# A decoder layer whose recurrent outputs go to two halves of the partitions, with GpSimd's tile arithmetic on VectorE and another meter for side work

## The chip, the core and the metric

One core of a Trainium2 chip runs the whole kernel. The metric is the device time of one execution in microseconds (us). A kernel is timed several times and the median is given; beside it stands one execution taken by the hardware profiler, from which all rows of the profile come.

## The reference

One decoder layer in float32 on 256 tokens of width 2048. A residual stream `x` passes three branches, each with a norm before and after:

```python
h = rms_norm(x, mix_pre_norm)
proj = h @ w_in                                  # 2048 x 10536
# mLSTM, 4 heads, from q, k, v, o and two gates  -> ha
# RWKV-7, 16 heads of 64: per token
#   S = S diag(w) - (S kk) (kk a)^T + v k^T ;  y = S r
# group norm of y, bonus, output gate            -> hb
merged = sigmoid(g_a) * (ha @ w_branch_a) + sigmoid(g_b) * (hb @ w_branch_b)
x = x + rms_norm(merged @ w_out, mix_post_norm)
x = x + rms_norm(cross_attention(rms_norm(x), rms_norm(mem)), xattn_post_norm)
u = rms_norm(x, ffn_pre_norm) @ w_up             # 2048 x 16384
uc = conv_b + causal_conv3(u)
x = x + rms_norm((gelu(uc_gate) * uc_up) @ w_down, ffn_post_norm)
```

## The kernel before

**The big products.** All weights are streamed from HBM in tiles of 128 x 1024 numbers (512 KB; 128 x 768 in the first block `sm`). To keep float32 precision, each number is split into a high part (ScalarE's cast to fp32r, tile `wh`, line 348) and a low part (VectorE's subtraction, tile `wl`, line 357); the activations are split likewise (`hh`/`hl`, `qh`/`ql`, `fh`/`fl`, `as`). Three TensorE products (high x high, high x low, low x high) add up in one PSUM bank. `raw`, the tile as loaded, has three buffers, `wh` and `wl` four each. TensorE's products, the side ones too, are all issued by the helper `mm` at line 181. In `fm` blocks a product has 256 columns (outputs by feature), in `tm` blocks 512 (by token).

**The order of the work.** `blocks` lists the big products: `sm` (small columns of `w_in`), `r`, `k`, `v` (two blocks each), `q` (two), `vm` and `o` (two each, `tm`), then the gates and branch products in turn, `w_mo`, the cross-attention products, 32 blocks `w_fu` and two `w_fd`. `run()` walks through them. For each weight tile it issues the split of the tile three ahead and the load of the tile six ahead, then TensorE's products of this one. A weight tile of an `fm` block is two half steps of 12 products each.

**Side work.** Everything else (scaling a block's result, gates, norms, the RWKV recurrence, softmax, residuals) is written as generators, and `yield` ends a piece. `Spread.half()` is called at every half step and decides which pieces are issued there. There are three lists: `bulk` (what follows a block, in order), `back` (long preparations: `sm_rest`, four `k_group`, `bonus`, `inverses`, `hb_split`) and `chains` (one piece each `chain` half steps: `gates`, `rwkv`, the squares of a residual). `Meter` books a price for each VectorE and ScalarE instruction (VectorE 70 + 1.04 ns an element, ScalarE 200 + 0.83). `half()` adds `RATE_D` and `RATE_A` to the two credits up to `CAP`; one piece of `bulk` or `back` is issued if both credits are above zero; a piece that books nothing passes on to the next in line. Chains run while both credits are above -700. GpSimd's work isn't booked. `side.need` and `side.until` issue a task's pieces at once where a block needs the result. Engines run their instructions in the order of issue, so a side product on TensorE that waits for VectorE holds the big products behind it.

**The places that the change touches.**

- `x_piece` (line 459) splits two rows of `x` and lets GpSimd square them and add them up (lines 464 to 468) for the first norm, whose row of rstd comes in `sm_evac` by `st0.finish`.
- `sm_rest` makes the low-rank decay and gate products (`zwa`) of RWKV; `gates` the mLSTM gates and the tile `pw`.
- `k_group` (lines 740 to 752) makes for two feature tiles the scaled vectors of the recurrence: `KR` and `BK`, in part on GpSimd. `head_sums` makes sums over a head by a TensorE product of a split tile (side products `ssk`, `bon`).
- `inverses` inverts the 32 x 32 triangular blocks, 31 steps of two VectorE instructions, two steps a piece.
- `rwkv(hf)` runs for each half of the heads over four chunks of 64 tokens, a step each three half steps: transposes (`bkt`) and `gram`, then `lv`, `X`, `U`, and last `Tn` (the next state) and `Y` (the output). `aux` is the pool of four side PSUM buffers. Of the two heads `e` of a pair, Tn goes to partitions `E2[e]` (0 to 63 or 64 to 127); Y goes for both heads to the partitions of the chunk, `cr = E2[c % 2]`, in two buffers `qy[e]`.
- `Residual` adds a branch to `x`, in eight parts: scale `z`, add to `xr` (GpSimd for parts 2 to 7), split into the next block's input. In the first residual (`early`, for the cross-attention) each part's square is added by GpSimd at once; in the second (for `w_fu`) the squares follow as a chain.
- `fd_evac` writes the result; one of eight pieces goes over ScalarE and GpSimd.

Of the kernel before, what the change touches and what calls it, by code (L numbers as in the profile page):

```python
# [15 lines left out]
P = 128  # L16
# [54 lines left out]
class Spread:  # L71


    RATE_D, RATE_A, CAP = 600.0, 820.0, 1200.0
# [28 lines left out]
    def half(self):  # L103
        self.tick += 1
        self.cd = min(self.cd + self.RATE_D, self.CAP)
        self.ca = min(self.ca + self.RATE_A, self.CAP)
# [39 lines left out]
def _layer(ctx, tc, nc, d, dbg):  # L146
# [95 lines left out]
    class Stat:  # L242
# [14 lines left out]
        def add(self, src, eng=None):  # L257
            if self.n == 0:
                self.start()
                act.activation(self.acc, src, AF.Square)  # L260
            else:
                q = self.square()
                act.activation(q, src, AF.Square)
                (eng or dve).tensor_add(self.acc, self.acc, q)  # L264
            self.n += 1
# [193 lines left out]
    def x_piece(c):  # L459
        for j in range(2):  # L460
            split_gain(hh[:, c * 2 + j], hl[:, c * 2 + j], xq[c][:, j], pcol("mixg", c * 2 + j))
        if c == 0:
            st0.start()
            pool.tensor_mul(st0.acc, xq[c], xq[c])
        else:
            q = st0.square()
            pool.tensor_mul(q, xq[c], xq[c])
            pool.tensor_add(st0.acc, st0.acc, q)
        st0.n += 1
# [4 lines left out]
    def pre_sm(ci, feed):  # L474
# [8 lines left out]
        if ci + 3 < 8:  # L483
            x_piece(ci + 3)
        if ci == 4:
            sp.dma_start(con, d["con"])
# [21 lines left out]
    def sm_evac(ps):  # L508
        dve.tensor_scalar(om, pcol("mu", 0, 27), -1.0, 1.0, op0=ALU.mult, op1=ALU.add)
        dve.tensor_scalar(oka, pcol("ka", 0, 8), -1.0, 1.0, op0=ALU.mult, op1=ALU.add)  # L510
        yield from st0.finish(3)
# [19 lines left out]
    def sm_rest(wa, gl0, gl1):  # L531
# [3 lines left out]
        for i, h in enumerate(hid):  # L535
# [5 lines left out]
            dve.tensor_sub(ul[E2[i]], up[E2[i]], uh[E2[i], i])  # L541
            yield
# [28 lines left out]
    def gates():  # L571
# [92 lines left out]
        for o in (0, 256):  # L664
            for e in range(2):
                v = pw[E2[e], :, o + e * 64:o + e * 64 + 64]
                pool.tensor_mul(v, v, bc(ccol("im", 64)[E2[e]], 4))
# [40 lines left out]
    def k_group(p0):  # L708
# [31 lines left out]
        pool.tensor_mul(KR8[:, :, 1], f8(rr[:, ss]), f8(ep))  # L740
# [4 lines left out]
        pool.tensor_mul(k2, kr, k2)  # L745
# [4 lines left out]
        for e in range(2):  # L750
            dve.tensor_mul(BK8[E2[e], :, e], f8(kk)[E2[e]], f8(nr)[E2[e]])
            pool.tensor_mul(BK8[E2[e], :, 1 - e], f8(k2)[E2[e]], f8(nr)[E2[e]])
# [5 lines left out]
    def head_sums(name, v):  # L758
# [4 lines left out]
        for _ in range(3):  # L763
# [7 lines left out]
    def inverses():  # L771
# [38 lines left out]
        act.copy(Lt, L.rearrange("p c i -> p i c"))  # L810
        yield
# [47 lines left out]
    def rwkv(hf):  # L859
# [12 lines left out]
        for c in range(4):  # L872
# [5 lines left out]
            if c < 3:  # L878
# [3 lines left out]
                act.copy(bkt, q)  # L882
            au = C("au", f"au{hf}", [P, 2, 2, 4, 64])
# [55 lines left out]
            qy = [aux("Y", [P, 4, 64]) for _ in range(2)]  # L939
            for j, e in heads():  # L940
                mm(qy[e][cr, j], gr[:, e, j], uv[:, e, j], start=(j == 0), stop=(c == 0))
            if c:
                for j, e in heads():
                    mm(qy[e][cr, j], KR[E2[e], p0 + j, c, 1], T[hf][E2[e], j], start=False)
            for e in range(2):
                act.copy(ye[cr, e], qy[e][cr])
# [92 lines left out]
    def mlstm():  # L1039
        pw, vm, so = M["pw"], M["vm"], M["so"]  # L1040
        M["pws"] = T2("pws")
        pool.tensor_add(M["pws"].rearrange("p a b -> p (a b)").rearrange("p (h q) -> p h q", h=4),
                        pw[:, :, 128:256], pw[:, :, 256:384])
# [143 lines left out]
    class Residual:  # L1187
# [8 lines left out]
        def run(self):  # L1196
# [27 lines left out]
            def add(i, eng):  # L1224
                eng.tensor_add(part(xr, i), part(xr, i), part(z, i))  # L1225
# [11 lines left out]
            for i in range(1, 8):  # L1237
                if i == 1:
                    add(1, dve)
                if i < 7:  # L1240
                    scale(i + 1)
                    add(i + 1, pool)
# [3 lines left out]
                if self.early:  # L1246
                    self.st2.add(part(xr, i - 1), pool)
                elif i == 6:
                    self.stats = side.add(self.squares(0), chain=1)
                yield  # L1250
            if self.early:
                self.stats = side.add(self.squares(7), chain=1)
                yield

        def squares(self, i0):
            for i in range(i0, 8):
                self.st2.add(part(M["xr"], i), pool)
# [312 lines left out]
    def fd_evac(n):  # L1570

        def gen(ps):
# [19 lines left out]
            def result(t, c):  # L1592
                f = slice(c % 2 * 512, c % 2 * 512 + 512)
                x, z_ = M["xt"][c // 2][:, t, f], M["z3", c // 2][:, t, f]
                if t and c == 1:
                    act.activation(z_, z_, AF.Copy, scale=rco[:, t:t + 1])
                    pool.tensor_add(x, x, z_)
                else:
                    dve.scalar_tensor_tensor(x, z_, rco[:, t:t + 1], x, op0=ALU.mult, op1=ALU.add)
# [124 lines left out]
```

## Time and profile before

| what | value |
|---|---|
| median of 3 runs | 1940.54 us (1940.47 to 1940.81) |
| profiled execution, its time | 1939.58 us |
| its span, first to last instruction | 1937.6 us |
| TensorE (PE) busy | 1900.6 us, 98% |
| VectorE (DVE) busy | 1326.1 us, 68% |
| ScalarE (ACT) busy | 1001.6 us, 52% |
| GpSimd (POOL) busy | 137.1 us, 7% |
| read from HBM | 347.73 MB, 181 GB/s over the span |
| mean granted TensorE clock | 0.995 |

A row of a group reads: line, engine, operation, out<-in, shapes, xcount, then busy us and mean ns of one, then the engine's idle time just ahead of it and who ended it. A row of a timeline begins with its start and its duration; merged rows carry a count. Overlapping instructions are merged, so a row's duration is up to the last one's end. A row of stretches reads `A:B length, busy time of each engine (xinstructions)`, then the granted TensorE clock, the share of the DMA engines and GB/s; narrowed to one engine it has that engine's time alone. A row of the chain of waits has start, duration and what it was.

### The profile page before, as it was taken

The numbers are of one execution on the slowest core, as the hardware profiler recorded it, in microseconds if no ns is written. First come the engines' busy times: TensorE is split into PE (matmuls) and PEld (weight loads), VectorE is DVE, ScalarE is ACT, GpSimd is POOL, SyncE is SP. The second block draws the span as 40 slices with busy tenths as digits, with TensorE's granted clock in tenths as the row PEclk, the third lists the DMA queues.
The fourth block names the chain that finished last, engine by engine and source line by source line (L and its number), as shares of the span: only waits on it lengthen the run. The fifth ranks groups of instructions, "written<-read, shape, count | busy, mean of one in ns | idle before, by whom it ended". The sixth has DMA issues, their size and how long they took to land.

```text
span 1937.6 us, 36532 instructions
## 1 busy us (share of the span) xinstructions
PE 1900.6 (98%) x15084; PEld 1798.7 (93%) x15084; DVE 1326.1 (68%) x1789; ACT 1001.6 (52%) x1434; POOL 137.1 (7%) x127
## 2 busy tenths in 40 slices
PE   7999999999999999899999999999999999999998
PEld 7999987999999999789999999999999998888886
DVE  7879886566566665867767666776667675556555
ACT  4776535544454565555555445544455454455553
POOL 4213100010100000304000000000000000000000
PEclk9999999999999999999999999999999999999999
DMA  6555555344465675435555555556555555655554
GB/s 200 177 163 165 185 164 162 110 142 142 157 183 185 209 261 185 157 133 171 182 186 191 195 196 192 191 190 200 191 194 189 195 195 195 215 192 192 194 195 152
DMA packets 97606, 352.20 MB, mean 182 GB/s; under 512 B 10880, under 2 KB 11136, under 8 KB 97056
## 3 DMA queue, kind: packets, MB, share of 16 engines
q1 hardware_dynamic: 96496, 348.07, 55.0%
q8 instruction: 118, 1.93, 0.4%
q10 hardware_dynamic: 720, 1.15, 0.2%
q0 software_dynamic: 224, 0.66, 0.1%
q14 instruction: 48, 0.39, 0.1%
HBM read 347.73 MB, written 2.10 MB: 181 GB/s over the span
## 4 chain that ended last, share of the span: by engine, by line
PE 87%; DVE 5%; ACT 2%; issue 2%; DMA 2%; POOL 1%; DVEq 0%; SPq 0%; ACTq 0%; POOLq 0%
PE fm L181 59%; PE tm L181 23%; DVE wl L357 2%; ACT wh L348 1%; DMA raw<-in_w_in_dram 1%; DVE fl L66 1%; PE Y L181 1%; DMA raw<-in_w_fu_dram 0%; PE gram L181 0%; PE lv L181 0%; DVE z L66 0%; POOL xr L1225 0%; POOL stx L264 0%; DMA x<-in_x_dram 0%; DVE BK L66 0%
## 5 line engine op out<-in xcount | busy, mean ns | idle before, releaser
L357 DVE TENSOR_TENSOR wl<-raw,wh 128x1024 fp32r<-128x1024 f32 (+1 forms) x648 | 809.6, 1251 | 448.5 <-ACT wh L348 445.4
L348 ACT CAST wh<-raw 128x1024 fp32r<-128x1024 f32 (+1 forms) x648 | 675.7, 1046 | 562.1 <-PE fm L181 373.2
L181 PE MATMUL fm<-fl,wh 128*128 128x256 f32 x2048 | 568.3, 278 | 1.0 <-DVE fl L66 1.0
L181 PE MATMUL fm<-fh,wh 128*128 128x256 f32 x2048 | 568.7, 278 | 0.2 <-ACT fh L66 0.2
L181 PE MATMUL fm<-fh,wl 128*128 128x256 f32 x2048 | 567.7, 277 | 0.0
L181 PEld LDWEIGHTS fm<-fl,wh 128*128 128x128 f32 x2048 | 386.0, 188 | 1.8 <-DVE fl L66 1.7
L181 PEld LDWEIGHTS fm<-fh,wh 128*128 128x128 f32 x2048 | 386.0, 188 | 0.5 <-ACT fh L66 0.5
L181 PEld LDWEIGHTS fm<-fh,wl 128*128 128x128 f32 x2048 | 386.0, 188 | 0.0
L181 PE MATMUL tm<-wh,as 128*128 128x512 f32 x1024 | 315.5, 389 | 0.0
L181 PE MATMUL fm<-hh,wl 128*128 128x256 f32 x1072 | 301.7, 281 | 11.9 <-DVE wl L357 11.9
L181 PE MATMUL fm<-hh,wh 128*128 128x256 f32 x1072 | 305.5, 285 | 1.1 <-ACT wh L348 1.1
L181 PE MATMUL fm<-hl,wh 128*128 128x256 f32 x1072 | 300.7, 280 | 0.0
L181 PEld LDWEIGHTS tm<-wh,as 128*128 128x128 f32 x1024 | 192.1, 188 | 39.8
L181 PEld LDWEIGHTS fm<-hh,wl 128*128 128x128 f32 x1072 | 203.8, 190 | 13.8 <-DVE wl L357 13.8
L181 PEld LDWEIGHTS fm<-hh,wh 128*128 128x128 f32 x1072 | 204.0, 190 | 4.1 <-ACT wh L348 1.5
L181 PEld LDWEIGHTS fm<-hl,wh 128*128 128x128 f32 x1072 | 204.2, 190 | 0.1
L181 PE MATMUL tm<-wl,as 128*128 128x512 f32 x512 | 199.3, 389 | 0.0
L181 PEld LDWEIGHTS tm<-wl,as 128*128 128x128 f32 x512 | 96.1, 188 | 20.0
L66 ACT CAST as<-ac 128x256 fp32r<-128x256 f32 x128 | 45.6, 404 | 112.9 <-PE tm L181 112.9
L66 DVE TENSOR_TENSOR as<-ac,as 128x256 fp32r<-128x256 f32 x128 | 48.6, 422 | 61.7 <-ACT as L66 61.6
L225 POOL TENSOR_TENSOR rco<-var,mhalf 128x1 f32<-128x1 f32 x2 | 1.1, 551 | 1011.6 <-DVE var L66 1011.6
L181 PE MATMUL fm<-mgh,wh 128*128 128x256 f32 x256 | 71.4, 279 | 0.0
(363 smaller groups left out, 2323.6 us busy)
## 6 DMA issues: line engine op xcount, KB each, us to landing
raw<-in_w_fu_dram SPq DMA_DIRECT2D x256, 512.0 KB, 4.2
raw<-in_w_in_dram SPq DMA_DIRECT2D x160, 512.0 KB, 3.7
raw<-in_w_fd_dram SPq DMA_DIRECT2D x128, 512.0 KB, 4.2
raw<-in_w_br_dram SPq DMA_DIRECT2D x32, 512.0 KB, 3.8
raw<-in_w_mo_dram SPq DMA_DIRECT2D x32, 512.0 KB, 4.3
raw<-in_w_xk_dram SPq DMA_DIRECT2D x8, 512.0 KB, 4.5
raw<-in_w_xq_dram SPq DMA_DIRECT2D x8, 512.0 KB, 3.6
raw<-in_w_xv_dram SPq DMA_DIRECT2D x8, 512.0 KB, 4.1
```

The costliest lines, as they stand in the source:

```text
L66: return f(out, *a, **k)
L181: pe.matmul(out, lhsT, rhs, start=start, stop=stop, skip_group_check=True)
L225: pool.tensor_tensor(out, v, mhalf[:, 0:out.shape[1]], op=ALU.pow)
L348: nc.scalar.copy(wh, r)
L357: nc.vector.tensor_sub(wl, r, self.st[self.nl][0])
```

## The change

It does seven things: (1) Y of both heads goes to one PSUM buffer, each head to its own half of the partitions, and ScalarE's copies bring both to the chunk's rows; (2) the tile arithmetic of GpSimd (squares and sums of squares, residual adds, parts of `k_group`, masks of `pw`, `pws`, one result) goes to VectorE, its squares to ScalarE, and is booked there; the small powers for rstd, copies and fills stay on GpSimd; (3) squares of the first norm come later, those of the first residual as a chain after part 6; (4) `RATE_D` rises from 600 to 740, and a credit below -700 is lifted to -700 ahead of each half step's addition; (5) more empty pieces stand ahead of side products: six for three in `head_sums`, five ahead of `zwa`; (6) a piece ends between `bkt` and `gram`; (7) the copy `Lt` is cut in two pieces.

```diff
@@ class Spread @@
-    RATE_D, RATE_A, CAP = 600.0, 820.0, 1200.0
+    RATE_D, RATE_A, CAP, DEBT = 740.0, 820.0, 1200.0, -700.0
@@ Spread.half @@
         self.tick += 1
-        self.cd = min(self.cd + self.RATE_D, self.CAP)
-        self.ca = min(self.ca + self.RATE_A, self.CAP)
+        self.cd = min(max(self.cd, self.DEBT) + self.RATE_D, self.CAP)
+        self.ca = min(max(self.ca, self.DEBT) + self.RATE_A, self.CAP)
@@ Stat.add @@
-        def add(self, src, eng=None):
+        def add(self, src):
...
                 act.activation(q, src, AF.Square)
-                (eng or dve).tensor_add(self.acc, self.acc, q)
+                dve.tensor_add(self.acc, self.acc, q)
@@ x_piece @@
             split_gain(hh[:, c * 2 + j], hl[:, c * 2 + j], xq[c][:, j], pcol("mixg", c * 2 + j))
-        if c == 0:
-            st0.start()
-            pool.tensor_mul(st0.acc, xq[c], xq[c])
-        else:
-            q = st0.square()
-            pool.tensor_mul(q, xq[c], xq[c])
-            pool.tensor_add(st0.acc, st0.acc, q)
-        st0.n += 1
@@ pre_sm @@
             x_piece(ci + 3)
+        else:
+            for c in range((ci - 5) * 2, (ci - 5) * 2 + 2):
+                st0.add(xq[c])
@@ sm_evac @@
         dve.tensor_scalar(oka, pcol("ka", 0, 8), -1.0, 1.0, op0=ALU.mult, op1=ALU.add)
+        for c in (6, 7):
+            st0.add(xq[c])
+            yield
@@ sm_rest @@
             dve.tensor_sub(ul[E2[i]], up[E2[i]], uh[E2[i], i])
             yield
+        for _ in range(5):
+            yield
@@ gates @@
                 v = pw[E2[e], :, o + e * 64:o + e * 64 + 64]
-                pool.tensor_mul(v, v, bc(ccol("im", 64)[E2[e]], 4))
+                dve.tensor_mul(v, v, bc(ccol("im", 64)[E2[e]], 4))
@@ k_group @@
         dve.tensor_mul(kk, kk, nr)
-        pool.tensor_mul(KR8[:, :, 1], f8(rr[:, ss]), f8(ep))
+        dve.tensor_mul(KR8[:, :, 1], f8(rr[:, ss]), f8(ep))
...
         pool.tensor_copy(pce[:, ss], ep.rearrange("p a (c t) -> p a c t", c=4)[:, :, :, 63])
-        pool.tensor_mul(k2, kr, k2)
+        dve.tensor_mul(k2, kr, k2)
...
             dve.tensor_mul(BK8[E2[e], :, e], f8(kk)[E2[e]], f8(nr)[E2[e]])
-            pool.tensor_mul(BK8[E2[e], :, 1 - e], f8(k2)[E2[e]], f8(nr)[E2[e]])
+            dve.tensor_mul(BK8[E2[e], :, 1 - e], f8(k2)[E2[e]], f8(nr)[E2[e]])
@@ head_sums @@
         split(h, l, v)
-        for _ in range(3):
+        for _ in range(6):
@@ inverses @@
         Lt = C("Lt", "au1", [P, 32, 32])
-        act.copy(Lt, L.rearrange("p c i -> p i c"))
-        yield
+        for i in (slice(0, 16), slice(16, 32)):
+            act.copy(Lt[:, i], L.rearrange("p c i -> p i c")[:, i])
+            yield
@@ rwkv: bkt and gram @@
                 act.copy(bkt, q)
+                yield
@@ rwkv: Y @@
             ye = ysb.rearrange("p (a b) v -> p b a v", b=2)
-            qy = [aux("Y", [P, 4, 64]) for _ in range(2)]
+            qy = aux("Y", [P, 4, 64])
             for j, e in heads():
-                mm(qy[e][cr, j], gr[:, e, j], uv[:, e, j], start=(j == 0), stop=(c == 0))
+                mm(qy[E2[e], j], gr[:, e, j], uv[:, e, j], start=(j == 0), stop=(c == 0))
...
                 for j, e in heads():
-                    mm(qy[e][cr, j], KR[E2[e], p0 + j, c, 1], T[hf][E2[e], j], start=False)
+                    mm(qy[E2[e], j], KR[E2[e], p0 + j, c, 1], T[hf][E2[e], j], start=False)
             for e in range(2):
-                act.copy(ye[cr, e], qy[e][cr])
+                act.copy(ye[cr, e], qy[E2[e]])
@@ mlstm @@
         M["pws"] = T2("pws")
-        pool.tensor_add(M["pws"].rearrange("p a b -> p (a b)").rearrange("p (h q) -> p h q", h=4),
-                        pw[:, :, 128:256], pw[:, :, 256:384])
+        dve.tensor_add(M["pws"].rearrange("p a b -> p (a b)").rearrange("p (h q) -> p h q", h=4),
+                       pw[:, :, 128:256], pw[:, :, 256:384])
@@ Residual.run: add @@
-            def add(i, eng):
-                eng.tensor_add(part(xr, i), part(xr, i), part(z, i))
+            def add(i):
+                dve.tensor_add(part(xr, i), part(xr, i), part(z, i))
@@ Residual.run, squares @@
                 if i == 1:
-                    add(1, dve)
+                    add(1)
...
                     scale(i + 1)
-                    add(i + 1, pool)
+                    add(i + 1)
...
                     side.more()
-                if self.early:
-                    self.st2.add(part(xr, i - 1), pool)
-                elif i == 6:
-                    self.stats = side.add(self.squares(0), chain=1)
-                yield
-            if self.early:
-                self.stats = side.add(self.squares(7), chain=1)
-                yield
-        def squares(self, i0):
-            for i in range(i0, 8):
-                self.st2.add(part(M["xr"], i), pool)
+                if i == 6:
+                    self.stats = side.add(self.squares(), chain=1)
+                yield
+        def squares(self):
+            for i in range(8):
+                self.st2.add(part(M["xr"], i))
@@ fd_evac: result @@
                 x, z_ = M["xt"][c // 2][:, t, f], M["z3", c // 2][:, t, f]
-                if t and c == 1:
-                    act.activation(z_, z_, AF.Copy, scale=rco[:, t:t + 1])
-                    pool.tensor_add(x, x, z_)
-                else:
-                    dve.scalar_tensor_tensor(x, z_, rco[:, t:t + 1], x, op0=ALU.mult, op1=ALU.add)
+                dve.scalar_tensor_tensor(x, z_, rco[:, t:t + 1], x, op0=ALU.mult, op1=ALU.add)
```

## Prediction

> **What bounds the kernel now.** I read the page's first part, then busy time by stretches of 20 us or a stage, then each engine's timeline in the stretches where TensorE loses time.
>
> ```profile
> PE 1900.6 (98%) x15084; PEld 1798.7 (93%) x15084; DVE 1326.1 (68%) x1789; ACT 1001.6 (52%) x1434; POOL 137.1 (7%) x127
> 1040.00:1240.00 200.00, 200.00 (x1761) 200.00 (x1760) 138.32 (x186) 100.39 (x129) 0.00 (x0) 1.00 0.58 192
> 6.70:66.00 59.30, 48.24 (x370) 45.94 (x370) 44.40 (x50) 30.46 (x46) 21.37 (x16) 0.94 0.62 186
> 100.00:300.00 200.00, 196.99 (x1527) 184.76 (x1527) 168.26 (x246) 110.62 (x149) 38.10 (x33) 1.00 0.54 168
> ```
>
> TensorE bounds it. From 1040 us on it takes a 256-column product every 200/1761 = 0.1136 us without a break, and nothing that the change does to the other engines can show there. Time can come from two things only: fewer or quicker TensorE instructions, and the stretches where TensorE starves. The worst of those is the head: 370 products in 59.3 us are worth 42 us, so 17 are lost. Others, shown below, lie around 425, 790-810 and 865-920 us. Except at 425, GpSimd works on full tiles in all of them.
>
> **A, the outputs Y: -4.1 us.** A chunk's 16 Y instructions on `gr` put both heads of a pair on the same 64 output partitions; the new form gives each head its own half, as the Tn products have it.
>
> ```profile
> 386.41 0.69 PE L181 MATMUL Tn<-au,bg 128*64 128x64 f32 x16
> 386.93 1.10 PE L181 MATMUL Y<-au,bg 128*64 128x64 f32 x16
> 387.96 0.68 PE L181 MATMUL Y<-T,KR 64*64 64x64 f32 x16
> 441.92 0.51 PE L181 MATMUL X<-T,KR 64*64 64x64 f32 x11
> ```
>
> From start to start, 16 Tn take 0.52 us and 16 Y of the same shape 1.03. The saving is 0.51 us for each of 4 chunks and two halves of the heads: 8 x 0.51 = 4.1, all on TensorE's path. Bounds: 0 (no pairing) to -4.1; I take -4.1, as the Tn row has exactly the new form. The 16 products Y<-T now write from two row halves into one PSUM bank. The X<-T row already does this, at some 0.03 us each ((0.51 - 0.2)/10), so I count nothing. The Trainium skill speaks against that step: TensorEngine Tiling (Array Packing), Restrictions and Gotchas, says that different row tiles can't access the same PSUM bank at once. By it the 96 Y<-T instructions would double, +3 us, and the sum would be -20; the X<-T row doesn't agree with the rule where the column halves differ too.
>
> **B, the squares of x leave GpSimd: -7.5 us.**
>
> ```profile
> 20.12 1.88 POOL L468 TENSOR_TENSOR st<-st,sq 128x512 f32<-128x512 f32 x1
> 26.39 1.34 POOL L468 TENSOR_TENSOR st<-st,sq 128x512 f32<-128x512 f32 x1
> 20.78 2.68 DVE L66 SCALAR_TENSOR_TENSOR hl<-x,par,hh 128x256 fp32r<-128x256 f32 x2
> 23.39 2.02 DVE L357 TENSOR_TENSOR wl<-raw,wh 128x768 fp32r<-128x768 f32 x1
> 25.33 2.68 DVE L66 SCALAR_TENSOR_TENSOR hl<-x,par,hh 128x256 fp32r<-128x256 f32 x2
> 28.81 0.87 DVE L66 SCALAR_TENSOR_TENSOR hl<-x,par,hh 128x256 fp32r<-128x256 f32 x2
> 31.26 0.94 DVE L357 TENSOR_TENSOR wl<-raw,wh 128x768 fp32r<-128x768 f32 x1
> 20.88 4.67 DMA raw<-in_w_sm_dram
> ```
>
> While GpSimd works, VectorE's pair of `hl` takes 2.68 us and `wl` 2.02; after GpSimd's last square they take 0.87 and 0.94. A step of the first block is 25.33 - 20.78 = 4.6 us, while TensorE needs 18 x 0.1136 = 2.05 for it. Each `wl` also frees the raw buffer for the next transfer, so the transfers come late too. Without GpSimd, VectorE needs some 1.7 us a step. Next late are the transfers: three buffers, each 4.67 landing + 0.94 and a cast of about as much, give 2.2 us a step. I take 2.4: from TensorE's first products (at 6.7 us, where the stretch above was cut) eight steps end near 26, where the last `wl` at 31.3 + 0.9 and 2 us of products now end near 34. That is -8. The squares come back on ScalarE (eight, 0.63 each by the meter's price, 0.2 + 0.00083 x 512) and VectorE (seven adds of 0.69, row in C), in the last three steps and in `sm_evac`, two pieces later for the row of rstd. They delay splits that TensorE wants three tiles later; +0.5. Bounds: -3 (transfers stay as slow) to -10 (144 products without a wait end at 23).
>
> **C, first residual (790-810 us): -5.**
>
> ```profile
> 783.00 1.46 POOL xr L1225
> 784.46 1.44 POOL stx L264
> 787.66 1.47 POOL xr L1225
> 792.00:796.00 4.00, 2.79 (x24) 1.00 0.40 131
> 782.85 1.90 DVE L66 SCALAR_TENSOR_TENSOR ql<-xr,par,qh 128x256 fp32r<-128x256 f32 x2
> 784.67 2.31 DVE L357 TENSOR_TENSOR wl<-raw,wh 128x1024 fp32r<-128x1024 f32 x1
> 814.82 1.22 DVE L357 TENSOR_TENSOR wl<-raw,wh 128x1024 fp32r<-128x1024 f32 x1
> L66 DVE TENSOR_TENSOR sty<-sty,sq 128x512 f32<-128x512 f32 x7 | 4.8, 687 | 0.9 <-ACT sq L66 0.9
> ```
>
> The chain of waits turns in 787.66 - 783.00 = 4.66 us a part: GpSimd's add and square sum, then `ql` and `wl`, both stretched. TensorE wants 24 x 0.1136 = 2.73 and gets 24 products in 4 us instead of 35; over 18 us that is 18 x 11/35 = 5.7 lost. After: two VectorE instructions of 0.6 (0.69 less an overlap of about 0.08), `ql` 0.8 (as `hl` alone, row in B) and `wl` 1.15 (the row at 814.82, GpSimd at rest) make 3.15 a part, and the first parts are done under the block ahead, which needs none. Left is about 0.7. Bounds: -3 to -6.5. The squares now follow as one piece each half step (0.6 beside 0.6 of `wl`, in 1.37). So stx comes some four half steps later than the parts allow; the value block's 24 us of products hide that. Without the cover it costs up to 4 x 1.37 = 5.5, which would eat the gain.
>
> **D, second residual (865-920 us): -4.**
>
> ```profile
> 882.48 0.68 DVE L66 TENSOR_TENSOR z<-z,stb 128x512 f32<-128x512 f32 x1
> 883.07 1.91 DVE L66 SCALAR_TENSOR_TENSOR fl<-xr,par,fh 128x256 fp32r<-128x256 f32 x2
> 886.04 0.68 DVE L66 TENSOR_TENSOR z<-z,stb 128x512 f32<-128x512 f32 x1
> 903.55 11.49 POOL L264 TENSOR_TENSOR stf<-stf,sq 128x512 f32<-128x512 f32 x6 [0.19 <-ACT sq L66]
> 912.00:916.00 4.00, 2.41 (x22) 1.00 0.63 213
> 916.00:920.00 4.00, 2.95 (x24) 1.00 0.71 243
> ```
>
> A part takes 886.04 - 882.48 = 3.56 and would take 3.15: 0.4 x 6 = 2.4. Then GpSimd sums squares for 11.49 us, TensorE's column of sums waits, and 46 products run where 70 fit: 2.7 lost, of which I give back 1.6. Bounds: -2 to -6.
>
> **E, the stall at 425 us: -3.**
>
> ```profile
> 427.10 1.13 PE L181 MATMUL gram<-KR,BK 64*128 64x128 f32 x14 [1.84 <-DVE bg L66]
> 428.96 0.41 PE L181 MATMUL fm<-hh,wh 128*128 128x256 f32 x1
> 429.18 0.41 PE L181 MATMUL fm<-hl,wh 128*128 128x256 f32 x1
> ```
>
> Both recurrences ask for three side PSUM buffers within one step; there are four. TensorE stands 1.84 us and then runs for about 3.3 us at 0.21 us a product, half speed, another 1.5. The new yield puts `gram` a step behind `bkt`, and Y holds one buffer, not two. Bounds: 0 to -3.4. Its price is three more steps of three half steps in each recurrence, 9 x 1.37 = 12 us. What waits for that is `hb`:
>
> ```profile
> 562.84 1.39 PE fm L181 x12
> L181 PE MATMUL fm<-hb,wh x256: 275/276/285, 578.8 to 667.0; 128*128 128x256 f32 x128
> ```
>
> The last zg products stand just ahead of 562.84, `hb` is first read at 578.8: 16 us of cover, more if the recurrence starts earlier.
>
> **F, the meter and the work moved in 100-300 us: +1.**
>
> ```profile
> L357 DVE TENSOR_TENSOR wl<-raw,wh 128x1024 fp32r<-128x1024 f32 x65 | 85.7, 1318 | 18.3 <-ACT wh L348 17.9
> L66 DVE TENSOR_TENSOR BK<-kt 64x512 f32<-64x512 f32 x8 | 10.5, 1309 | 0.3
> L66 DVE TENSOR_TENSOR kt<-kt,at 128x512 f32<-128x512 f32 x4 | 4.9, 1237 | 0.1
> ```
>
> A group of K gives VectorE four more instructions of 0.6, four groups 9.6 us, the masks of `pw` four of some 0.35: 11. Gone is the stretching: `wl` 65 x (1.318 - 1.22) = 6, `BK` 8 x 0.62 = 5, `kt` 4 x 0.55 = 2: 13. So the demand stays at 168 of 200 us. But the meter lets it come denser: 0.74 + 0.62 (half a `wl`) per half step of 1.37, and debt beyond -0.7 is forgiven, so every half step runs a piece. Two pieces of each group now cost 2.4 us, of which 1.44 is paid (8 x 0.96 = 8 forgiven), and those of `inverses` cost up to 1.34 by its prices, where 0.74 comes in. TensorE has three split tiles in hand, 8.2 us. It lost 200 - 196.99 = 3 us here; I take 4 after, with bounds 0 to 11 (F: -3 to +8). The longer waits ahead of side products (3 to 6 half steps in `head_sums`, 5 ahead of zwa) cost TensorE nothing, since a piece that does nothing passes the half step to the next in line; they keep TensorE from waiting for a VectorE that is now up to 8 us behind. The halved copy `Lt`: 0.
>
> **G, the end: -0.3.**
>
> ```profile
> 1931.16 3.08 DVE L66 SCALAR_TENSOR_TENSOR xt<-z,rco,xt 128x512 f32<-128x512 f32 x3
> 1928.84 1.41 DVE L66 SCALAR_TENSOR_TENSOR xt<-z,rco,xt 128x512 f32<-128x512 f32 x2
> ```
>
> Three results beside GpSimd take 3.08 us, two alone 1.41; four alone 2.8.
>
> **Sum:** -4.1 - 7.5 - 5 - 4 - 3 + 1 - 0.3 = -22.9. The profiled span is 1937.6, its run 1939.58, the median 1940.54; 1940.5 - 22.9 = 1917.6.
>
> **Rivals.** (1) *VectorE becomes the bound between 100 and 250 us; slower.* Forgiven debt (8 + at most 16 x 0.6 in `inverses`) puts VectorE up to 17.6 us behind; less the 8.2 in hand, TensorE stands 9.4. If it stands in nine pieces, each followed by the half speed that the rows at 428.96 and 429.18 show (+1.5 each, 13.5), it pays 23 and the gain is gone: 1941; from ten stalls on it is slower, and with twelve, 27 us, the time is 1945. For it: VectorE is at 168 of 200 already. Against: while GpSimd stretched it, it was as full, and TensorE lost 3 us. The Trainium skill (TensorE: Matmul & The Clock Gate, Part 1) has the half speed come after gaps of over some 3.4 us, by which these short stalls would cost no more than themselves, 9.4, and the sum would be -14; the row at 427.10 shows it after 1.84. (2) *The head stays bound by its transfers*, B at -3 or nothing: 1921 to 1925. For it: 4.67 us a landing; against: they are issued late because `wl` is late. (3) *The residuals give nothing*, as late squares or transfers take the place of GpSimd: 1926.5. Against: the z, ql and wl rows stretch only beside GpSimd. (4) *The Y pairs don't overlap*, or row halves wait for their one bank: 1921 to 1922. The X<-T row speaks against the second, the Tn row against the first.
>
> **Chances.** Forecast (1917.6, own range 1910 to 1924) 0.55; (2) 0.15; (3) 0.12; (4) 0.04; (1) 0.14, of which 0.09 is slower. All good bounds together give 1940.5 - 33 = 1907, the bad ones of B to F 1936. The range 1908 to 1932 leaves out part of (1) and little else. A measurement of this kernel can tell about 0.2%, 3.9 us: faster 0.86, same 0.05, slower 0.09.
>
> **What the new profile would show.** A: 16 Y from start to start in 0.52. B: `hl` pairs at 0.87 throughout, the first w_in products near 26 us. C and D: parts every 3.2 us, no GpSimd there. E: no stop before gram. F: inverses done well ahead of 300 us, VectorE near 20 of 20 us; if TensorE loses over 10 us in 100:300, F was wrong, and with it most likely the sum.

## The result: 16.5 us faster, 6.4 less than forecast

The changed kernel takes 1923.99 us in the median of four runs (1921.08 to 1925.74) against 1940.51 for the kernel before on the same chip, a ratio of 0.9914 (95% interval 0.9901 to 0.9927). The gain is 16.5 us where 22.9 were forecast. The profiled execution is the slowest of the four (1925.74 us, span 1923.9). Its busy times on the profile's page:

```profile
PE 1894.1 (98%) x15084; PEld 1791.1 (93%) x15084; DVE 1310.1 (68%) x1844; ACT 1004.8 (52%) x1440; POOL 38.8 (2%) x64
```

VectorE has taken over GpSimd's work, 55 instructions more, and is busy 16 us less: 1310.1 for 1326.1. Two groups of VectorE between 100 and 250 us show where that comes from:

```profile
L358 DVE TENSOR_TENSOR wl<-raw,wh 128x1024 fp32r<-128x1024 f32 x49 | 59.6, 1220 | 17.8 <-ACT wh L349 17.5
L66 DVE TENSOR_TENSOR BK<-kt 64x512 f32<-64x512 f32 x16 | 10.3, 683 | 0.4
```

`BK` has twice the instructions in the same busy time (16 of 683 ns for 8 of 1309), and `wl` takes 1220 ns where it took 1318 between 100 and 300 us. Now the head, first in the kernel before and then after, as busy time by stretches:

```profile
6.40:35.00 28.60, 20.41 (x144) 19.31 (x145) 26.71 (x24) 12.88 (x23) 19.81 (x14) 0.88 0.57 186
```

```profile
6.40:35.00 28.60, 25.98 (x207) 24.56 (x207) 22.85 (x37) 20.94 (x35) 0.00 (x0) 1.00 0.79 258
53.00:86.00 33.00, 29.91 (x226) 28.26 (x225) 26.03 (x44) 24.18 (x39) 13.28 (x20) 0.95 0.47 160
100.00:300.00 200.00, 196.66 (x1527) 181.94 (x1526) 168.48 (x270) 106.27 (x141) 6.17 (x12) 1.00 0.52 167
768.00:797.00 29.00, 27.16 (x216) 26.37 (x215) 25.23 (x37) 16.66 (x24) 0.70 (x1) 0.94 0.52 182
851.00:908.00 57.00, 52.43 (x424) 50.45 (x424) 46.45 (x75) 35.09 (x55) 1.40 (x2) 0.97 0.44 147
```

In the first 28.6 us TensorE does 207 products for 144. Three of them are the small sums `st`; the other 60 are worth 60 x 0.1136 = 6.8 us. The other four rows are stretches of the changed kernel that still lose time. VectorE's timeline in the head, and then TensorE's, with the rows of Tn and Y and the stops of the other stretches:

```profile
19.38 0.88 DVE L66 SCALAR_TENSOR_TENSOR hl<-x,par,hh 128x256 fp32r<-128x256 f32 x2
21.85 0.96 DVE L358 TENSOR_TENSOR wl<-raw,wh 128x768 fp32r<-128x768 f32 x1 [1.59 <-ACT wh L349]
```

```profile
379.44 0.69 PE L182 MATMUL Tn<-au,bg 128*64 128x64 f32 x16
379.96 0.64 PE L182 MATMUL Y<-au,bg 128*64 128x64 f32 x16
380.52 0.68 PE L182 MATMUL Y<-T,KR 64*64 64x64 f32 x16
64.92 0.38 PE L182 MATMUL fm<-hh,wl 128*128 128x256 f32 x1 [2.59 <-DVE wl L358]
278.23 0.50 PE L182 MATMUL tm<-wl,hh 128*128 128x512 f32 x1 [1.39 <-DVE wl L358]
282.30 0.50 PE L182 MATMUL tm<-wl,hh 128*128 128x512 f32 x1 [1.06 <-DVE wl L358]
791.44 0.58 PE L182 MATMUL st<-ones,stx 128*128 128x1 f32 x4 [1.84 <-DVE stx L66]
876.59 0.38 PE L182 MATMUL fm<-fh,wl 128*128 128x256 f32 x1 [1.66 <-DVE wl L358]
```

`hl` takes 0.88 us a pair and `wl` 0.96. Sixteen Y on `au` take 0.56 us from start to start (1.03 before). Each of the five stops waits for VectorE: in the second `r` block, twice in the inverses, and in both residuals. GpSimd has no part in them: it is at rest in the last four, and the `wl` ahead of the first takes 1.21 us beside its copies of small rows.

**Where the gain is made and lost.** The lead of a block is the start of its first big product in the kernel before, less the start in the kernel in question, found by counting the big products in the two traces (every trace has the same 15084 products, so the counts match). Each column is one execution. The columns behind the first are the experiments below, by what is done in them.

| lead in us at | changed | no floor | head only | floor from 64 | floor to 336 | floor 65-336 | third in line |
|---|---|---|---|---|---|---|---|
| first r block | 8.1 | 10.3 | 10.0 | 8.7 | 10.0 | 9.5 | 10.2 |
| first k block | 2.6 | 12.0 | 12.9 | 10.2 | 6.2 | 10.8 | 12.1 |
| block behind the first on hb | 12.2 | 13.1 | 14.4 | 15.9 | 15.8 | 16.5 | 18.7 |
| kx, ahead of residual 1 | 11.2 | 13.1 | 14.4 | 15.9 | 15.8 | 16.5 | 18.7 |
| second wo block | 13.1 | 19.2 | 15.0 | 17.4 | 21.8 | 22.3 | 24.9 |
| fourth fu block, after residual 2 | 12.5 | 22.7 | 12.8 | 17.2 | 25.0 | 25.8 | 28.4 |

The changed kernel has its 8 us at the head, loses 5.5 of them in the r blocks, gains 9.6 up to the block behind the first on `hb`, and then gets 1.9 from the first residual and -0.6 from the second, where 5 and 4 were forecast. A lead differs between executions: up to `hb` the kernel of the column "floor to 336" runs the changed kernel's program, loses 3.8 us in the r blocks, and leads by some 2 to 3.5 us more up to there. The residuals differ by more than that. Four kernels have the floor there (the changed kernel, floor from 64, without the patience, without the yield); they get 1.5 to 3.4 us from the first residual and -0.2 to -1.0 from the second. The five without it behind half step 336 (no floor, floor to 336, floor 65-336, third in line, K groups on GpSimd) get 5.8 to 6.3 and 3.2 to 3.5.

### The profile page after: what moved, and what is told of

Same layout as the page of the kernel before. It is cut to its first block, busy times and chain, and to the rows that moved or that the text cites. A ratio compares the mean times of both kernels' runs of the same rounds, so it can differ in the third digit from the quotient of the medians.

```text
span 1923.9 us, 36535 instructions
## 1 busy us (share of the span) xinstructions
PE 1894.1 (98%) x15084; PEld 1791.1 (93%) x15084; DVE 1310.1 (68%) x1844; ACT 1004.8 (52%) x1440; POOL 38.8 (2%) x64
## 4 chain that ended last, share of the span: by engine, by line
PE 87%; DVE 6%; DMA 3%; ACT 2%; issue 1%; POOL 0%; SPq 0%; DVEq 0%; POOLq 0%; ACTq 0%
PE fm L182 61%; PE tm L182 22%; DVE wl L358 2%; DMA raw<-in_w_mo_dram 1%; ACT wh L349 1%; DMA raw<-in_w_sm_dram 1%; DMA raw<-in_w_in_dram 1%; DVE tmp L66 1%; DVE z L66 0%; PE gram L182 0%; DVE L L66 0%; PE Y L182 0%; DVE fl L66 0%; PE lv L182 0%; DVE ql L66 0%
## 5 line engine op out<-in xcount | busy, mean ns | idle before, releaser
L358 DVE TENSOR_TENSOR wl<-raw,wh 128x1024 fp32r<-128x1024 f32 (+1 forms) x648 | 787.5, 1220 | 470.9 <-ACT wh L349 468.0
L182 PE MATMUL fm<-mgh,wl 128*128 128x256 f32 x256 | 71.3, 278 | 0.7 <-DVE wl L358 0.7
```

The costliest lines, as they stand in the source:

```text
L182: pe.matmul(out, lhsT, rhs, start=start, stop=stop, skip_group_check=True)
L358: nc.vector.tensor_sub(wl, r, self.st[self.nl][0])
```

## The experiments

Theory: the meter's new floor costs the missing time. `half()` forgives debt beyond 700 ns before it adds the credit, so a task whose pieces cost more than a half step still issues one at every half step, and ScalarE or VectorE falls behind TensorE. Rival: the demand is what it is, and the moved work costs its time wherever it is put. A half step named in a text is a position in the program's order, which is fixed when the program is built.

**No floor, and the old meter.**

```
no floor:   RATE_D, RATE_A, CAP, DEBT = 740.0, 820.0, 1200.0, -1e9
old meter:  RATE_D, RATE_A, CAP, DEBT = 600.0, 820.0, 1200.0, -1e9
```

> The changed kernel with DEBT at minus infinity, so that no debt is forgiven; the higher VectorE rate stays. Theory (the forgiven debt lets each half step issue a piece, so VectorE and ScalarE fall behind and TensorE pays in the r block, in the inverses and in the second residual): 6 to 9 us faster than the changed kernel, 1915 to 1918; the stops of 1.39 and 1.06 us on wl between 275 and 292 us are gone, and TensorE reaches the first gram later than 292.8. Rival (the floor is harmless, the demand on VectorE is what it is, and the moved work costs the same wherever it is put): within 2 us of the changed kernel's 1924.

> The changed kernel with the old meter (VectorE rate 600, no floor). Theory (the meter is the part of the change that loses time): as without the floor, 1915 to 1919, with the inverses ending later, near 300 us, where they did before. Rival (the moved work needs a higher rate, since VectorE's booked work has grown by 11 us between 100 and 250 us): the inverses come too late and the blocks behind them wait, 1927 or more.

Without the floor: 1916.21 us (ratio to before 0.9877, interval 0.9863 to 0.9890), 7.8 less than the changed kernel and outside its interval. The theory's size is met, and the table places it: 9.4 more lead than the changed kernel at the k block, and 6.1 and 3.5 us from the two residuals. The two stops on `wl` in the inverses are gone, and the first `gram` of the recurrence comes at 313.7 us instead of 292.8, as expected. It is not free. The lead falls again at `hb`, where TensorE's timeline has

```profile
559.25 0.50 PE L182 MATMUL zg<-gs,gwh 128*128 128x256 f32 x2 [2.97 <-ACT gwh L66]
```

The recurrence comes late, the program forces the last 11 pieces of `hb_split` at the start of the block that reads it, and that block, from the last big product ahead of it, takes 22.7 us for 11.2.

With the old meter: 1974.24 us (1.0177, 1.0162 to 1.0191). The theory expected 1915 to 1919 and fails by 55 us; the rival's direction holds. Of TensorE's busy time and its timeline:

```profile
556.00:616.00 60.00, 33.79 (x359) 30.23 (x359) 26.99 (x48) 20.22 (x41) 5.60 (x6) 0.69 0.16 47
```

```profile
568.70 1.09 PE L985 MATMUL yT<-con,ysb 128*128 128x128 f32 x4 [6.74 <-DVE ysb L66]
```

The moved instructions are booked now, GpSimd's were not. At 600 ns a half step the inverses end at half step 243 (185 before), and 26 pieces of the recurrence and 15 of `hb_split` are left when `hb` is needed. They run one behind the other (the stop of 6.74 us comes a second time at 587.89) with nothing beside them, at a granted clock of 0.69. So a higher rate belongs to the moved work; the floor is what costs.

**The floor in part of the program.**

```
        if 64 < self.tick <= 336:          # or one of the two bounds alone
            self.cd, self.ca = max(self.cd, self.DEBT), max(self.ca, self.DEBT)
        self.cd = min(self.cd + self.RATE_D, self.CAP)
        self.ca = min(self.ca + self.RATE_A, self.CAP)
```

> The changed kernel with debt forgiven only from half step 65 on, so that the blocks sm, r and half of k run without a floor. Theory (in the r blocks the floor forgives ScalarE's debt of up to 2.6 us that sm_rest has run up, so its casts come denser than ScalarE can follow and TensorE loses 7 us in r1): r1 takes 26 us instead of 33 and the k block starts 12 us before the unchanged kernel's instead of 2.6; 1924 - 7 = 1917. Rival (what the r block wins is lost again at the inverses, which stay under the floor): 1921 to 1924.

> The changed kernel with debt forgiven only until half step 336, where the recurrence's result is needed; from there on, both residuals run without a floor. Theory (under the floor a part of the residual is issued at every half step, 2.4 us of VectorE where 1.4 us pass): the first residual gives 6 us instead of 1.7 and the second 3 instead of -0.6; 1924 - 8 = 1916. Rival (VectorE's work in the residuals is the same and only moves): 1922 to 1925.

> Debt forgiven between half steps 65 and 336 alone: both of the edits before together. Theory (the floor helps only where the recurrence has to be in time, and without it there hb is 11 us late): 1924 - 7 - 8 = 1909, better than with no floor at all (1916.2), with hb_split done ahead of its block and no stop there. Rival (the two overlap, or no floor at all loses nothing at hb that the floor doesn't lose in the inverses): 1914 to 1917.

From 65 on: 1920.12 (0.9897, 0.9882 to 0.9912), 3.9 less than the changed kernel, though the intervals overlap. The second r block takes 25.9 us instead of 33.1, and the stop of 2.59 us on `wl`, behind 4.5 us of VectorE's rows for the gates and the norm's scaling, isn't there; but of the 7.6 us of lead at the k block 3.9 are gone again (+5.7 up to the block behind the first on `hb`, for 9.6 in the changed kernel). With the floor `sm_rest` is done at half step 54, without it at 60, so about half of the time lost in the r block seems to be work done earlier; that is read from the leads of single executions, not tested.

Until 336: 1915.31 (0.9873, 0.9859 to 0.9888), 8.7 less, outside the interval, as expected. The residuals give 6.1 and 3.2 instead of 1.9 and -0.6. Busy time in the stretches that answer to the last two shown above (they begin 4 and 9 us earlier here):

```profile
764.00:793.00 29.00, 29.00 (x226) 27.84 (x225) 27.40 (x39) 19.23 (x27) 0.00 (x0) 1.00 0.64 198
842.00:899.00 57.00, 55.66 (x450) 54.29 (x449) 44.37 (x67) 31.32 (x48) 1.39 (x2) 0.94 0.51 167
```

VectorE is about as busy (27.4 for 25.2 us, 44.4 for 46.5), and TensorE does more. In the first stretch it does 22 products of 512 columns more (0.227 us each) and 5 of 256 fewer, worth 4.4 us; in the second it does 33 big products of 256 columns more, worth 3.7 (the rows count side products too). What differs is the order. VectorE's timeline in the second residual, in the changed kernel and then here:

```profile
871.08 0.68 DVE L66 TENSOR_TENSOR z<-z,stb 128x512 f32<-128x512 f32 x1
873.20 0.68 DVE L66 TENSOR_TENSOR z<-z,stb 128x512 f32<-128x512 f32 x1
875.32 1.22 DVE L358 TENSOR_TENSOR wl<-raw,wh 128x1024 fp32r<-128x1024 f32 x1
```

```profile
863.12 0.68 DVE L66 TENSOR_TENSOR z<-z,stb 128x512 f32<-128x512 f32 x1
865.23 1.22 DVE L360 TENSOR_TENSOR wl<-raw,wh 128x1024 fp32r<-128x1024 f32 x1
866.36 0.68 DVE L66 TENSOR_TENSOR z<-z,stb 128x512 f32<-128x512 f32 x1
```

With the floor two parts stand between two `wl`, and TensorE waits for the later one at 876.59; without it there is a `wl` behind each part. In the first residual the chain of waits of the changed kernel runs over a transfer:

```profile
783.21 1.23 DVE wl L358
784.46 4.11 DMA raw<-in_w_xv_dram
788.65 1.06 ACT wh L349
789.73 1.23 DVE wl L358
790.96 0.34 DVE stx L66
```

A `wl` that comes late frees its `raw` buffer late, the next tile lands late, and the last sum for stx stands behind that tile's cast and `wl`; TensorE waits for it at 791.44. With the floor to 336 no cast between 774 and 800 us waits for a transfer. The rival has the same work moved to another place; the place decides what waits behind it.

Both together: 1913.73 (0.9866, 0.9851 to 0.9881), 10.3 less than the changed kernel where 15 were expected, and 2.5 less than with no floor at all, which the intervals don't tell apart. `hb` is in time. The inverses, still under the floor, keep their stop:

```profile
273.94 0.50 PE L184 MATMUL tm<-wl,hh 128*128 128x512 f32 x1 [1.40 <-DVE wl L360]
```

**The parts one by one.** Y alone on the kernel before (`qy = aux(...)`, `qy[E2[e], j]`), and the head alone (`x_piece` without GpSimd, the squares as in the change):

> The kernel before with the new place of Y alone: one buffer, each head of a pair on its own half of the partitions. Theory: 16 Y<-au,bg from start to start in 0.52 us instead of 1.03, 8 x 0.51 = 4.1 us less, 1936.4. Rival (two halves of the rows that write to one PSUM bank take turns): the 96 Y<-T products double, +3 us, 1939.5. A third outcome, below 1935: the buffer that Y gives back also shortens the stall ahead of gram at 427 us (1.84 us and as much again at half speed).

> The kernel before with the squares of x alone moved from GpSimd to ScalarE and VectorE (three last steps of the first block and its evacuation). Theory (GpSimd's stretching of VectorE was the head's bound): the r block starts 8 us earlier and most of it stays to the end, 1932 to 1934. Rival (what the head gains is given back where sm_rest's casts and rows now meet the r block's casts): the lead is 8 us at the start of the r block and 3 or less at the start of the k block, 1937 to 1939.

Y alone: 1936.38 (0.9981, 0.9972 to 0.9990), 3.9 less for 4.1 expected.

```profile
385.54 0.64 PE L181 MATMUL Y<-au,bg 128*64 128x64 f32 x16
386.11 0.68 PE L181 MATMUL Y<-T,KR 64*64 64x64 f32 x16
424.81 1.13 PE L181 MATMUL gram<-KR,BK 64*128 64x128 f32 x14 [2.10 <-DVE bg L66]
```

Sixteen Y in 0.57; the 16 Y<-T on two row halves in one bank take 0.68 as before. The buffer that Y gives back doesn't shorten the stop ahead of `gram`: 2.10 us for 1.84.

The head alone: 1926.86 (0.9933, 0.9921 to 0.9946), 13.4 less; both theories had less. The lead is 10.0 at the first r block, 12.9 at the k block and 14.4 behind the recurrence; the rival has it given back at the k block, and it isn't. Behind the head, a row of the kernel before shows a stop of TensorE that this kernel lacks; busy time by stretches has the same 37 us in both, before first:

```profile
169.39 0.38 PE L181 MATMUL fm<-hh,wl 128*128 128x256 f32 x1 [2.23 <-DVE wl L357]
```

```profile
155.00:192.00 37.00, 34.77 (x299) 34.58 (x298) 35.66 (x39) 25.04 (x38) 14.91 (x12) 1.00 0.55 171
```

```profile
155.00:192.00 37.00, 37.00 (x324) 37.00 (x323) 34.53 (x44) 24.90 (x37) 9.99 (x8) 1.00 0.61 187
```

In both GpSimd works in the K groups; before, the `wl` that TensorE waits for stands behind three stretched entries of VectorE's timeline (2.34, 1.77 and 2.27 us). With the blocks 12 us earlier the two don't meet. That the shift is the reason is inferred from the timelines, not tested.

**The meter alone, and the change without its patience.** The first is the kernel before with the two lines of the meter. The second leaves out the five empty pieces ahead of zwa and three of the six in `head_sums`. It also leaves out the `yield` that the kernel before has in that place, so ahead of zwa it is less patient than the kernel before.

> The kernel before with the new meter alone (VectorE rate 740, debt beyond 700 ns forgiven). Theory (before, the old meter had the recurrence done in time, so an earlier one buys nothing, while the denser work costs TensorE in the r block, the inverses and the residuals): 3 to 10 us slower than before, 1943 to 1950. Rival (side work that is done earlier takes the stops out of the later blocks): 1936 or less. Neither: within 3 us of 1940.

> The changed kernel without the patience: no six half steps ahead of zwa, three instead of six in head_sums. The program then ends sm_rest at half step 43 instead of 54 and hb_split at 319 instead of 333. Theory (the patience keeps TensorE from waiting at zwa and at the head sums, and delays the rest by work that nobody waits for): stops on uh, ul, hsh or hsl of 1 to 4 us in the r and k blocks, 1925 to 1928. Rival (the burst of ScalarE's casts in r1 is what costs, and it comes with the patience just as well): within 2 us of 1924 or faster.

The meter alone: 1968.37 (1.0145, 1.0128 to 1.0162), 28 us slower; slower was expected, by a third of that at most. Its profiled execution is 7 us behind the kernel before at the first k block, 18 behind the first block on `hb`, and 30 after the second residual. Two of its stops in TensorE's timeline, in the r blocks and in the first value block:

```profile
60.88 1.23 PE L181 MATMUL zwa<-xw,uh 128*128 128x256 f32 x4 [5.04 <-ACT uh L66]
172.04 0.58 PE L181 MATMUL ssk<-hsl,bones 128*128 128x256 f32 x1 [6.15 <-DVE hsl L66]
```

With denser pieces, a side product is issued only a few half steps behind the split that it reads, while ScalarE and VectorE are that far behind. The second kernel shows the first of these again:

```profile
52.78 1.22 PE L182 MATMUL zwa<-xw,uh 128*128 128x256 f32 x4 [5.49 <-ACT uh L66]
```

It has another of 2.27 us on hsl, and takes 1927.57 (0.9933, 0.9920 to 0.9945), 3.6 more than the changed kernel as expected, though the intervals overlap. The moved work needs the new rate. That the new meter needs the patience is shown by the stops (5.04 us with the spacing of the kernel before), not yet by the time. The parts don't add up: alone, the meter loses 28 us, and the change on the old meter 34.

**The yield ahead of gram.**

```
                 act.copy(bkt, q)
-                yield
```

> The changed kernel without the new yield between bkt and gram. Theory (the yield is what removed the stall of 1.84 us ahead of gram at 425 us, since three side buffers were asked for in one step): the stall and the half speed behind it come back in part, 1 to 3.4 us slower, 1925 to 1927. Rival (Y in one buffer alone gives the fourth buffer that was missing): 1922 to 1924, with hb done 14 half steps earlier, which nobody waits for.

1925.49 (0.9924, 0.9912 to 0.9936), 1.5 more: in the theory's range, but not told apart from no effect. The stop that the theory had isn't the one that came: there is none around 425 us, but one at the first `gram`.

```profile
290.40 1.64 PE L182 MATMUL gram<-KR,BK 64*128 64x128 f32 x16 [2.07 <-ACT bg L66]
```

In the changed kernel TensorE has no stop above 0.6 us between 288 and 520 us.

**A third in line, and the K groups back on GpSimd.** What the floor bought was the time of `hb`. The inverses wait behind two `bonus` tasks that mostly wait out half steps, and only two entries of `back` may issue. The second kernel has, besides, the multiplications of the K groups on GpSimd.

```
-        for s in self.bulk[:1] + self.back[:2]:      # and DEBT = -1e9
+        for s in self.bulk[:1] + self.back[:3]:
```

> The changed kernel with no debt forgiven, and with three instead of two entries of the list back in line for a piece, so that the inverses go on while the two bonus tasks wait out their half steps. The program then ends the inverses at half step 189 (199 without the third, 178 in the changed kernel) and forces 2 pieces of hb_split instead of 11. Theory (with no floor the only loss is the 11 us of the late hb): 1916 - 9 = 1907, the first product on hb without a stop of several us. Rival (what the late side work saves ahead of 550 us is only put off, and comes back when it is done earlier): 1912 to 1915, like the floor between 65 and 336 (1913.7).

> The best kernel so far (no debt forgiven, three of the list back in line; 1911.1) with the four multiplications of each K group back on GpSimd, where the meter doesn't book them. Theory (GpSimd stretches VectorE's instructions beside it, which cost TensorE 3 us between 100 and 250 us in the kernel before): wl back from 1.22 to about 1.35 us there, BK from 0.68 to 1.31, and 1 to 6 us slower, 1912 to 1917. Rival (VectorE has room there as long as the meter doesn't issue more than it books, and with 10 us less booked the program ends the inverses at half step 178 instead of 189 and hb_split at 328 instead of 336): the same or up to 4 us faster, 1907 to 1911.

The third in line: 1911.12 us (0.9851, 0.9836 to 0.9866), the lowest median of all, 29 less than before and 13 less than the changed kernel; 5.1 less than with no floor alone, where 9 were expected (these two intervals just overlap), and not told apart from the floor between 65 and 336. It lies between the two expectations, 4 above the one and 1 below the other. The inverses run without the two long stops; one of 0.53 is left. The K groups back on GpSimd: 1914.64 (0.9865, 0.9849 to 0.9882), 3.5 more, with overlapping intervals. The traces differ clearly, though. Busy time of the kernel with the third in line, and then of the one with GpSimd, with two of its VectorE groups and a stop of TensorE:

```profile
100.00:250.00 150.00, 150.00 (x1277) 143.97 (x1276) 125.50 (x184) 85.47 (x118) 6.14 (x12) 1.00 0.58 176
```

```profile
100.00:250.00 150.00, 147.13 (x1267) 141.64 (x1267) 130.78 (x184) 84.69 (x118) 34.41 (x28) 1.00 0.55 167
```

```profile
L358 DVE TENSOR_TENSOR wl<-raw,wh 128x1024 fp32r<-128x1024 f32 x48 | 62.9, 1315 | 12.6 <-ACT wh L349 12.3
L66 DVE TENSOR_TENSOR BK<-kt 64x512 f32<-64x512 f32 x8 | 10.6, 1326 | 1.4 <-POOL kt L747 1.2
```

```profile
158.44 0.39 PE L182 MATMUL fm<-hh,wl 128*128 128x256 f32 x1 [0.76 <-DVE wl L358]
```

With 184 instructions in that stretch, though not all the same ones, VectorE is busy 5.3 us longer (`wl` takes 1315 ns and `BK` 1326, for 1220 and 683 in the changed kernel), and TensorE loses 2.9 us that it doesn't lose otherwise. What the earlier `hb` (half step 328 for 336) gives back isn't separated from this.

## Why the prediction was right and where it was wrong

The direction was right, and so were the mechanisms of A and B. What failed is the cover that was to hide the late squares in C and D, and that the floor was priced for 100 to 300 us alone. That the time still lies within the forecast's own range of 1910 to 1924, at its very edge, is in part luck: B alone gave 5.9 us more than its term, and the floor outside its stretch took 10.3.

**A, right.** -4.1 forecast, -3.9 measured alone. The Tn row gave the price: Y needs 0.56 us, 0.04 more than forecast. The rule of one PSUM bank (the Trainium skill, TensorEngine Tiling (Array Packing), Restrictions and Gotchas) would, as an estimate, have doubled the time of 16 Y<-T; they take 0.68 us in one bank as in two.

**B, right in its mechanism, too small alone.** A step of 2.4 us and the first `w_in` products near 26 were forecast; they come at 25.0 in the head alone and 27.0 in the changed kernel (25.1 in the kernel with the floor to 336, which runs the same program there). Not in the sum were 2.9 us in the r blocks, where three stops on `wl` of 0.4 to 0.8 us shrink to one of 0.7, and the stop of 2.23 us at 169 us. The term ended where the block ended, and a later start changes what meets behind it too. In the changed kernel the floor took that part back.

**C and D, the steps that failed.** -5 and -4 were forecast, -1.9 and +0.6 came; without the floor it is -6 and -3. The price of a part, 3.15 us, was right: with the floor two parts of the first residual with one `wl` between stand 3.25 apart (`xr` at 773.50 and 776.75), and no `ql` or `wl` is stretched. The failure lies in what was put beside them. The prediction named the price ("Without the cover it costs up to 4 x 1.37 = 5.5") and judged the cover good, as the value block's products hide a late stx. But under the floor the column sums of stx are issued as early as their pieces, not as early as VectorE gets to them. They stand in TensorE's queue ahead of the last twelve products of the query block, so the value block, which was to hide the wait, comes behind them. TensorE meets them at 791.44, stands 1.84 us and soon runs at half the granted clock for 3.41 us (below). What held VectorE there was a late transfer, as the chain of waits shows. In the second residual it is the two parts ahead of one `wl`. Rival (3), late squares or transfers in GpSimd's place, is thus what happened, by the floor and not by the squares themselves, as the same squares without the floor give 6.1 us.

**E, not settled.** A and E together were to give 7.1; from the first g block to the one after `hb` the lead grows from 4.9 to 12.2. Without the yield it grows by as much (7.5), but there is the stop at 290 us ahead of it, and the time moves by no more than can be measured. The buffer that Y gives back doesn't remove the stop at 425 us alone (2.10 us there). What does remove it isn't shown.

**F, right in its place and wrong in its reach.** TensorE loses 200 - 196.66 = 3.3 us between 100 and 300, where 4 were forecast, and up to 250 us it isn't idle at all, so rival (1) is out. The sign named for a wrong sum, over 10 us lost there, didn't come, and the sum was still 6.4 us off:

```profile
100.00:250.00 150.00, 150.00 (x1302) 145.16 (x1302) 124.69 (x184) 85.21 (x118) 6.17 (x12) 1.00 0.53 173
```

The term failed because it was worked out for 100 to 300 us alone. The floor holds at every half step: the debts of `sm_rest` and `gates` in the r blocks (up to 2.6 us of ScalarE by the meter's book) and those of both residuals are forgiven too. Outside the half steps 65 to 336 the floor costs 10.3 us, which no term had. The parts without it, A 3.9 alone, B 13.4 alone, C 6.1 and D 3.2 by the leads, make 26.6; less 10.3 that is 16.3, beside the 16.5 measured. So close an agreement is partly chance: these come from different runs, E, F and G are left out, and each is good to some 2 us. The patience was counted at nothing; what the new meter costs without it (5.04 us at zwa, with the meter alone) no row of the kernel before could show.

**G.** Four results alone were to take 2.8 us; the last VectorE row of them is

```profile
1917.85 2.74 DVE L66 SCALAR_TENSOR_TENSOR xt<-z,rco,xt 128x512 f32<-128x512 f32 x4
```

## What to carry to other kernels

A meter that spreads side work should not forgive what it has booked without need: here, issue that ran ahead of the engine moved the wait to TensorE (1.84 us at 791.44, 1.66 at 876.59). Only in the stretch where one task had to be in time did it do no harm that could be measured. Letting that task pass those that are waiting out their steps did at least as well as raising the pace of all (1911.1 and 1913.7 us, not told apart). A rule that acts in a common helper is priced in every stretch that calls it, not in the one for which it seems made; and parts that lose alone (28 and 34 us) may gain together.

## What the hardware showed

**The granted clock after a stop does not follow from the stop's length alone.** After the stop of 1.84 us at 791.44, and after the one of 2.59 us at 64.92, the clock is halved; after the one of 1.39 us in the inverses, and after the one of 2.23 us at 169 us in the kernel before, it stays full. The traces show what differs. In the changed kernel the clock is halved from 66.04 to 69.45 us, from 793.08 to 796.49, from 854.52 to 857.93, and at the end. The first three starts are 727.04 and 61.44 us apart, 213 and 18 times 3.413 us, and each of these stretches is 3.41 us long: the clock changes on a fixed grid. Busy time taken along this grid, in the changed kernel:

```profile
62.63:66.04 3.41, 1.12 (x9) 1.13 (x10) 3.27 (x8) 0.56 (x1) 1.91 (x1) 1.00 0.03 11
66.04:69.45 3.41, 3.41 (x18) 3.41 (x17) 3.31 (x7) 2.81 (x5) 1.81 (x3) 0.50 0.50 187
789.67:793.08 3.41, 1.64 (x14) 1.67 (x15) 2.23 (x3) 1.08 (x2) 0.00 (x0) 1.00 0.63 235
793.08:796.49 3.41, 3.41 (x12) 2.83 (x11) 1.86 (x3) 1.05 (x1) 0.70 (x1) 0.50 0.69 231
```

And in the kernel before, where the half speed that the prediction shows at 428.96 begins at 428.14 and sets the grid:

```profile
165.32:168.73 3.41, 1.84 (x17) 1.65 (x15) 3.23 (x4) 0.00 (x0) 1.51 (x1) 1.00 0.37 142
168.73:172.14 3.41, 2.75 (x24) 2.75 (x25) 3.41 (x6) 1.85 (x3) 0.00 (x0) 1.00 0.50 154
172.14:175.55 3.41, 3.41 (x33) 3.41 (x32) 3.41 (x7) 3.06 (x6) 0.00 (x0) 1.00 0.73 197
```

The stop of 1.84 us lies almost whole in one step of the grid and leaves TensorE busy for less than half of it; the next step has half the clock. The stop of 2.23 us falls on an edge, both its steps are busy for more than half, and the clock stays full. So it counts where a stop falls, which differs from execution to execution. Idle time in a step isn't all: the half speed at 854.52 follows a step with 2.71 us busy, and a step with 1.57 us busy at 912.84 in the kernel before is followed by the full clock. What else counts isn't settled here.

The Trainium skill (TensorE: Matmul & The Clock Gate, Part 1) has the half speed come after gaps of over some 3.4 us. The row at 789.67 us doesn't agree, as the only stop in it is 1.84 us long.
